# A Trainium2 residual block: the casts of the mixer's first weight blocks moved three units later and one unit later

## The chip, the cores and the metric

The kernel runs on one core of a Trainium2 chip. The metric is the device time of one execution in microseconds (us), median over runs. The core has five engines that run their own instruction queues in order: TensorE (PE in the profile, its weight loads PEld), VectorE (DVE), ScalarE (ACT), GpSimd (POOL) and SyncE (SP). In this kernel SP only issues loads from and stores to HBM; POOL issues accumulating transfers and does a few small operations.

## The reference

One layer of a streaming-encoder block on 512 rows of 1024 columns, all in float32:

```python
h = h + 0.5 * _swiglu(_rmsnorm(h, ffn1_norm[i]), ffn1_w_in[i], ffn1_w_out[i])
z = _rmsnorm(h, mix_norm[i]) @ w_in[i]
conv_a, conv_gt, q, k, v, r, g_lr = jnp.split(z, SPLIT_POINTS, axis=-1)
y_conv = _conv_module(conv_a, conv_gt, conv_w[i], conv_b[i], conv_ln_g[i], conv_ln_b[i])
y_gla = _gla(q, k, v, r, g_lr, gate_w_up[i], gate_b[i], gla_norm[i])
h = h + jnp.concatenate([y_conv, y_gla], axis=-1) @ w_out[i]
h = h + 0.5 * _swiglu(_rmsnorm(h, ffn2_norm[i]), ffn2_w_in[i], ffn2_w_out[i])
gate = jax.nn.sigmoid(_rmsnorm(h, ple_norm[i]) @ ple_w_gate[i])
h = h + gate * (p[i] @ ple_w_proj[i])
```

The SwiGLU layers have 2816 inner columns. `w_in` has 1024 rows; its columns 0 to 511 are conv_a (the value of the convolution's GLU), 512 to 1023 conv_gt (its gate), then come q, k, v, r and the low-rank gate. The change touches the passage from the first SwiGLU layer to the product with `w_in`.

## The kernel before, in words

**Products in three passes.** A float32 product is made of reduced-precision passes. Each operand is split in a high part (`act.copy` to float32r) and a low part (the difference), and `mm3` makes three matmuls: high by high, high by low, low by high. For weights the high part is cast by ACT (`high`), and the low part is made in one of two ways: by a DVE subtraction (`low`; `parts` is both steps), or by `added`: ACT writes the raw weights times -1, rounded like the high part, and POOL issues a transfer that adds the raw weights to it, which leaves raw minus high. Which way is taken is written at each place.

**Buffers.** A load (`load`, `fetch`, line 233, issued on SP) goes into a raw buffer `wr`; there are six in all. A raw buffer is free once its last reader is done: the DVE subtraction, or the landing of the POOL transfer. High and low parts of most weights go to `wh` and `wl`, six each. The first weight blocks of the mixer are made ahead by `ahead`: it loads 128 columns of all 1024 rows (512 KB) for each block and splits them with `high4` in two tiles of four row blocks each, into `big` tiles called `wa`, of which there are 20 in the pool that also holds rows and activations. So one block of 128 columns is one load, two casts and two ACT instructions by -1 of 128x512, and two POOL transfers of 256 KB; `ahead(w_in, c, 2 * P)` makes two blocks.

**The first SwiGLU layer.** `ffn` works on pairs of 256 inner columns, eleven in all (0 to 10), most of them with seven products of sums of blocks instead of eight (units m1, m2, m6, m7, m5, m4, m3). The result goes through the output weights in `second`, in cuts of the inner columns; the last cut, columns 16 to 21 in units of 128, is in two parts of three: a first half of units "last",0, 2, 4 and a second half of units "rest",0, 2, 4, 6 and 7, each for two column blocks of h and each with its own load of 384 KB. The last pair's order is m1, m2, m6, m7, m5, "last",0, m4, m3, "last",2, "last",4, "rest",0, "rest",2, "rest",4, "rest",6, "rest",7. Each of the "last" and "rest" units is 18 matmuls of 512 columns. The second half needs the activations of the last pair, made by `act_parts` from m3's result; the "rest" units finish two blocks of h each: DVE adds them to h, ACT makes the high part `hg` for the mixer, DVE its low part, ACT squares h and DVE adds the squares to `sqacc` (`norm.add`).

**Order.** `drive` writes the units down in turn: a unit's own jobs first (its load was ordered seven units ahead, its cast and subtraction are ordered four units ahead of it), then the first thing left by the unit before, the unit's products with its hook, and what else was left. `hooks` maps a unit to work that is put in at its end of products. In `piece` of `second` the hook comes after the h rows and their `hg` casts, and ahead of the low parts and squares. PE, DVE and ACT keep this order through `Ordered` (line 46), within one part of the kernel; the mixer begins a new order (`in_order(True)` at line 1053), and its instructions may be placed by the scheduler between those of the layer's end. SP and POOL have no such order written by hand: a load is issued in turn as soon as a buffer is free for it.

**The mixer's begin.** `wb, wa = w_ahead` takes the gate's first two blocks (wb, columns 512 to 767) and the value's first two (wa, columns 0 to 255). The products are `pb0` with wb[0], `pa0` with wa[0], `pb1` with wb[1], `pa1` with wa[1], 24 matmuls each. In pa0 stand the column sums of sqacc, from which the row scale comes; `spread` of it stands in pb1. Further weights (`raw_b`, `raw_a`, `raw_q`, `raw_k`) are loaded by SP behind wa, and cast by ACT into w2b, w2a, wq and wk.

Of the kernel before, what the change touches and what calls it, by code (L numbers as in the profile page):

```python
# [15 lines left out]
P = 128  # L16
SEQ = 512
D = 1024
DC = D // P
DFF = 2816  # L20
D_CONV = 512
# [41 lines left out]
def block_kernel(ctx: ExitStack, tc: tile.TileContext, a: dict, out: bass.AP):  # L63
# [26 lines left out]
    def bt2(dt=F32R, s="a"):  # L90
        t = big.tile([P, 2, SEQ], dt, tag="A", bufs=NA, name=nm(s))
        hi, lo = t[:, 0], t[:, 1]
        whole_of[id(hi)] = hi, t
        return hi, lo
# [133 lines left out]
    def raw(nk, ncol):  # L228
        return wp.tile([P, 1024], F32, tag="raw", bufs=6, name=nm("wr"))[:, :nk * ncol].rearrange(
            "p (k c) -> p k c", k=nk)  # L230

    def fetch(r3, src, k0, nk, c0, ncol):
        nc.sync.dma_start(out=r3, in_=src[k0 * P:(k0 + nk) * P, c0:c0 + ncol].rearrange("(k p) c -> p k c", p=P))

    def load(src, k0, nk, c0, ncol):
        r3 = raw(nk, ncol)
        fetch(r3, src, k0, nk, c0, ncol)
        return r3
# [16 lines left out]
    def added(w):  # L255

        h3, l3, r3 = w
        act.mul(l3, r3, -1.0)
        pool.dma_start(out=l3.bitcast(F32), in_=r3, accum_op=ALU.add)
        return w  # L260
# [10 lines left out]
    def ahead(src, c0, ncol):  # L271


        return [[added(w) for w in high4(load(src, 0, DC, c, P))] for c in range(c0, c0 + ncol, P)]

    def high4(r3):

        w = []
        for k in range(0, DC, 4):
            hi, lo = (t.rearrange("p (k c) -> p k c", k=4) for t in bt2(s="wa"))  # L280
            act.copy(hi, r3[:, k:k + 4])
            w.append((hi, lo, r3[:, k:k + 4]))
        return w
# [355 lines left out]
    def constants():  # L639
        _, cwrow, gwurow = made  # L640
        gwu = cp.tile([P, 2 * P], F32, name="gwu")
        act.copy(gwu, gwurow)
        cw = cp.tile([P, 4 * WIDTH], F32, name="cw")
        ps = aux()
        for c in range(4):
            pe.transpose(ps[:, c * WIDTH:(c + 1) * WIDTH], cwrow[:, c * P:(c + 1) * P], ident[:WIDTH, :WIDTH])
        dve.tensor_copy(cw, ps[:, 0:4 * WIDTH])
        mean = cp.tile([P, P], F32, name="mean")
        pool.memset(mean, 1.0 / D_CONV)
        m1, m2 = (bt(s="m1")[:, 0:4 * CH].rearrange("p (c t) -> p c t", t=CH) for _ in range(2))  # L650
        mask = cp.tile([P, 4, CH], I32, name="mask")
        pool.memset(m1, 1.0)
        pool.memset(m2, 1.0)
        pool.affine_select(out=m1, in_=m1, compare_op=ALU.is_gt, fill=0.0, base=0,
                           pattern=[[0, 4], [-1, CH]], channel_multiplier=1)
        pool.affine_select(out=m2, in_=m2, compare_op=ALU.is_gt, fill=0.0, base=-CH,
                           pattern=[[0, 4], [-1, CH]], channel_multiplier=1)
        pool.tensor_copy(mask[0:CH], m1[0:CH])
        pool.tensor_copy(mask[CH:P], m2[CH:P])
        nbias = cp.tile([P, 2], F32, name="nbias")  # L660
        for j in range(2):
            dve.tensor_scalar(nbias[:, j:j + 1], vec("gate_b", j), -1.0, None, ALU.mult)
        made[:] = cw, gwu, mean, mask, nbias
# [359 lines left out]
    w_in = a["w_in"][0]  # L1023
    w_ahead = []

    def sums_hooks(x, names, at):

        h = {}
        for name, key in zip(names, at):
# [6 lines left out]
                  ("h4", 1): lambda *_: [steps[4](), xb.split("t2")],  # L1036
                  ("h5", 1): lambda *_: [xb.split("t3"), w2.s12()]})
    hooks.update({("m5", 3): lambda *_: made[0](), ("m3", 3): lambda *_: constants(),
                  ("m4", 10): lambda *_: w_ahead.append(ahead(w_in, D_CONV, 2 * P)),
                  ("last", 4): lambda *_: w_ahead.append(ahead(w_in, 0, 2 * P))})  # L1040
    FAR = {("h5", 1): 3, ("m1", 2): 3}
    CASTS = {("h5", 1): 4, ("m1", 2): 4}
    ADDS = {("h4", 1), ("m2", 2)}
# [77 lines left out]
    rs, rsb = mid  # L1121
# [427 lines left out]
    for k in range(4):  # L1549
        for n in range(3):  # L1550
            w, ps = half[n]
# [329 lines left out]
    rs = norm.rows()  # L1881
# [98 lines left out]
```

## Time and profile before

| | |
|---|---|
| median of three runs | 934.96 us (933.71 to 935.58) |
| the profiled execution | 934.95 us |
| its span, first to last instruction | 933.1 us |
| granted TensorE clock, mean | 0.997 |
| HBM read and written | 93.61 MB, 2.10 MB |

In the rows of the timeline a line has its start in us from the span's begin, its length in us, the engine, the line of the kernel, the operation, output and input tiles by name with their shapes, the count, and in brackets the idle time of the engine before it and what ended that. All operations pass through one helper, line 46, so they are told apart by their tiles. In rows where several instructions are merged, the length is from the first's start to the last's end. Output `wa` is the high or low part of the mixer's first blocks (both wb and wa of the code have the tile name `wa`), `wr` a raw weight buffer, `act` the activations' parts, `hg` the parts of the rows for the next layer, `pd` and `ps` are accumulators.

### The profile page before, as it was taken

The page shows a single profiled execution, that of the slowest core. Times are in us where ns is not written, and L with a number is a line of the kernel's source. Part 1 is how long each engine was busy: PE and PEld are TensorE (multiplying, and loading weights), DVE is VectorE, ACT ScalarE, POOL GpSimd, SP SyncE. Part 2 cuts the span into 40 slices and gives each one's busy share as a digit, 9 for nine tenths or more (in the row PEclk, how much of TensorE's full clock was granted, in tenths as well). Part 3 has the DMA queues.
Part 4 walks back from the last instruction along what each step waited for, and adds up shares of the span by engine and source line. Part 5 has one row for each costly group of instructions (what it writes and reads, how often), then busy time and mean ns, then how long its engine had stood idle before and what let it go on. Part 6 is the DMA issues. An engine that isn't in the chain of part 4 may idle for free.

```text
span 933.1 us, 12990 instructions
## 1 busy us (share of the span) xinstructions
PE 923.0 (99%) x5011; PEld 785.3 (84%) x5011; DVE 826.6 (89%) x1107; ACT 509.7 (55%) x745; POOL 56.9 (6%) x74
## 2 busy tenths in 40 slices
PE   9999999999999999999999999999999999999996
PEld 7898888888888878788877889888888888888885
DVE  6799989999999776999987789999999999997896
ACT  5874445445544574463564875355445444456883
POOL 0100100000000021001030020000000000000131
PEclk9999999999999999999999999999999999999998
DMA  7643333233432594346552654333223422348463
GB/s 231 186 112 113 116 113 113 74 108 113 124 87 66 153 237 116 77 111 161 137 124 79 158 115 134 113 113 116 89 90 122 126 89 79 110 132 245 92 111 115
DMA packets 108129, 114.37 MB, mean 123 GB/s; under 512 B 5203, under 2 KB 96517, under 8 KB 108068
## 3 DMA queue, kind: packets, MB, share of 16 engines
q1 hardware_dynamic: 101748, 94.67, 33.0%
q0 software_dynamic: 6304, 18.88, 11.2%
q8 instruction: 39, 0.64, 0.3%
q14 instruction: 22, 0.18, 0.1%
q10 hardware_dynamic: 16, 0.00, 0.0%
HBM read 93.61 MB, written 2.10 MB: 103 GB/s over the span
## 4 chain that ended last, share of the span: by engine, by line
PE 96%; DVE 2%; ACT 1%; DMA 1%; issue 0%; POOLq 0%; DVEq 0%; ACTq 0%
PE ps L46 58%; PE pd L46 38%; DMA wr<-in_w_in 1%; DVE wl L46 1%; DVE sq L46 0%; DVE g L46 0%; ACT act L46 0%; ACT wa L46 0%; ACT wh L46 0%; DVE u L46 0%; DVE rs L46 0%; ACT yc L46 0%; DVE y L46 0%; DVE s L46 0%; DVE act L46 0%
## 5 line engine op out<-in xcount | busy, mean ns | idle before, releaser
L46 DVE TENSOR_TENSOR wl<-wr,wh 128x1024 fp32r<-128x1024 f32 (+2 forms) x161 | 188.6, 1182 | 18.6 <-ACT wh L46 18.5
L46 ACT CAST wh<-wr 128x1024 fp32r<-128x1024 f32 (+2 forms) x178 | 176.4, 1022 | 21.6 <-PE ps L46 6.4
L46 PE MATMUL pd<-hg,wh 128*128 128x512 f32 x576 | 150.0, 391 | 0.0
L46 PE MATMUL ps<-act,wh 128*128 128x512 f32 x448 | 138.8, 391 | 0.5 <-ACT act L46 0.3
L46 PEld LDWEIGHTS pd<-hg,wh 128*128 128x128 f32 x576 | 106.1, 188 | 20.7 <-DVE u L46 0.3
L46 PE MATMUL ps<-hg,wh 128*128 128x512 f32 (+1 forms) x448 | 117.7, 347 | 0.1
L46 PE MATMUL pd<-t,wh 128*128 128x512 f32 x392 | 98.3, 393 | 0.0
L46 PEld LDWEIGHTS ps<-act,wh 128*128 128x128 f32 x448 | 83.1, 188 | 17.7 <-ACT act L46 0.7
L46 ACT ACTIVATE s<-g 128x512 f32<-128x512 f32 x48 | 30.3, 632 | 117.7 <-DVE g L46 117.7
L46 ACT COPY sq<-pd 128x1024 f32<-128x1024 f32 x45 | 45.8, 1017 | 86.7 <-PE pd L46 52.4
L46 PEld LDWEIGHTS ps<-hg,wh 128*128 128x128 f32 x448 | 78.0, 190 | 11.7 <-issue 1.3
L46 PE MATMUL ps<-act,wl 128*128 128x512 f32 x224 | 87.2, 389 | 0.0
L46 PE MATMUL pd<-hg,wl 128*128 128x256 f32 (+1 forms) x544 | 83.9, 289 | 0.0
L46 PEld LDWEIGHTS pd<-hg,wl 128*128 128x128 f32 x544 | 75.9, 190 | 6.3
L46 PEld LDWEIGHTS pd<-t,wh 128*128 128x128 f32 x392 | 70.6, 189 | 12.5
L46 PE MATMUL ps<-hg,wl 128*128 128x512 f32 (+1 forms) x224 | 77.1, 344 | 0.0
L46 ACT CAST wh<-sm 128x1024 fp32r<-128x1024 f32 x42 | 44.1, 1051 | 57.1 <-DVE sm L46 50.9
L46 DVE SCALAR_TENSOR_TENSOR cv<-glu,cw,cv 128x502 f32<-128x502 f32 (+24 forms) x90 | 61.9, 734 | 0.3
L46 PEld LDWEIGHTS pd<-t,wl 128*128 128x128 f32 x392 | 53.5, 191 | 3.8
L46 DVE TENSOR_TENSOR sq<-pd,sq 128x1024 f32<-128x1024 f32 x45 | 54.8, 1219 | 0.8 <-PE pd L46 0.8
L46 DVE TENSOR_TENSOR wl<-sm,wh 128x1024 fp32r<-128x1024 f32 x42 | 51.1, 1220 | 5.0 <-ACT wh L46 5.0
L46 PE MATMUL ps<-wh,hg 128*128 128x512 f32 x176 | 54.8, 393 | 0.0
(322 smaller groups left out, 1638.5 us busy)
## 6 DMA issues: line engine op xcount, KB each, us to landing
wr<-in_ffn_w_in SPq DMA_DIRECT2D x84, 512.0 KB
wr<-in_ffn_w_out SPq DMA_DIRECT2D x32, 512.0 KB
wr<-in_w_in SPq DMA_DIRECT2D x20, 512.0 KB
wl<-wr POOLq DMA_DIRECT2D x18, 512.0 KB, 5.2
wr<-in_ffn_w_out SPq DMA_DIRECT2D x16, 384.0 KB
wr<-in_w_out SPq DMA_DIRECT2D x8, 512.0 KB
wq<-in_ple_w_gate SPq DMA_DIRECT2D x8, 512.0 KB
wl<-wq POOLq DMA_DIRECT2D x8, 512.0 KB, 4.6
```

Source lines behind the costliest of these rows:

```text
L46: inst = call(*args, **kwargs)
```

## The change

The first two blocks (wb) are still loaded in the hook of m4 of pair 10, but only loaded. Their casts, the instructions by -1 and POOL's transfers come in the hook of "last",4, three units later. The other two blocks (wa), loads and all, go from the hook of "last",4 to that of "rest",0, the first unit of the second half. The number of instructions of every kind is the same.

```diff
@@ -271,7 +271,11 @@
     def ahead(src, c0, ncol):
 
 
-        return [[added(w) for w in high4(load(src, 0, DC, c, P))] for c in range(c0, c0 + ncol, P)]
+        return prepared([load(src, 0, DC, c, P) for c in range(c0, c0 + ncol, P)])
+
+    def prepared(rs):
+
+        return [[added(w) for w in high4(r3)] for r3 in rs]
 
     def high4(r3):
 
@@ -1036,8 +1040,9 @@
                   ("h4", 1): lambda *_: [steps[4](), xb.split("t2")],
                   ("h5", 1): lambda *_: [xb.split("t3"), w2.s12()]})
     hooks.update({("m5", 3): lambda *_: made[0](), ("m3", 3): lambda *_: constants(),
-                  ("m4", 10): lambda *_: w_ahead.append(ahead(w_in, D_CONV, 2 * P)),
-                  ("last", 4): lambda *_: w_ahead.append(ahead(w_in, 0, 2 * P))})
+                  ("m4", 10): lambda *_: w_ahead.append([load(w_in, 0, DC, D_CONV + i * P, P) for i in range(2)]),
+                  ("last", 4): lambda *_: w_ahead.append(prepared(w_ahead.pop())),
+                  ("rest", 0): lambda *_: w_ahead.append(ahead(w_in, 0, 2 * P))})
     FAR = {("h5", 1): 3, ("m1", 2): 3}
     CASTS = {("h5", 1): 4, ("m1", 2): 4}
     ADDS = {("h4", 1), ("m2", 2)}
```

One thing beside the places: before, each block's load was followed by its own casts; after, `ahead` writes both loads first and then the casts of both.

## The prediction, made before the changed kernel ran

> **What bounds the kernel now.** I read the totals first, then TensorE by unit, then the chain of waits around the change, and last the rows of ScalarE (ACT), VectorE (DVE), SP and TensorE (PE) there.
>
> ```profile
> span 933.1 us, 12990 instructions
> PE 923.0 (99%) x5011; PEld 785.3 (84%) x5011; DVE 826.6 (89%) x1107; ACT 509.7 (55%) x745; POOL 56.9 (6%) x74
> ```
>
> PE is busy for 923.0 of 933.1 us, so only what makes PE wait can be won. The units around the edit, as stretches of PE time (start:end, length, PE busy and count, clock, DMA share, GB/s):
>
> ```profile
> 322.27:330.46 8.19, 8.19 (x39) 1.00 0.80 140
> 330.46:335.61 5.15, 4.66 (x19) 1.00 1.13 281
> ```
>
> The first row is units "last",2 and "last",4, two times 18 matmuls: 4.10 us a unit. The second is "rest",0, with as many matmuls, and it takes 5.15: 1.05 us are lost. The clock is 1.00 in both. The chain of waits says why (start, length, what):
>
> ```profile
> 318.42 5.70 DMA wr<-in_w_in
> ...
> 326.34 0.73 ACT wh L46
> ...
> 327.10 0.96 DVE wl L46
> 328.06 0.61 DVE g L46
> ...
> 329.30 0.95 DVE wl L46
> 330.26 0.61 DVE m L46
> ...
> 330.89 0.63 ACT act L46
> ...
> 331.55 0.70 DVE act L46
> ```
>
> The load of the second w_in block holds ACT; behind it stand the cast for "rest",2, m3's silu path (g, m) and the splits of the last pair's activations, which "rest",0 reads from its fourth matmul on. ACT's own rows:
>
> ```profile
> 318.84 1.14 ACT L46 CAST wa<-wr 128x512 fp32r<-128x512 f32 x2 [2.42 <-DMA wr<-in_w_in]
> ...
> 324.15 1.14 ACT L46 CAST wa<-wr 128x512 fp32r<-128x512 f32 x2 [3.11 <-DMA wr<-in_w_in]
> ...
> 326.25 0.82 ACT L46 CAST wh<-wr 128x768 fp32r<-128x768 f32 x1
> 326.97 0.57 ACT L46 COPY g<-pd 128x512 f32<-128x512 f32 x1
> ...
> 333.46 1.14 ACT L46 CAST wa<-wr 128x512 fp32r<-128x512 f32 x2 [0.69 <-DMA wr<-in_w_in]
> ...
> 337.64 1.77 ACT L46 CAST wh<-wr 128x768 fp32r<-128x768 f32 x2
> ```
>
> There is a second place. "rest",7 ends at 351.93, where the mixer's first block begins:
>
> ```profile
> 351.93 6.52 PE L46 MATMUL ps<-hg,wa 128*128 128x512 f32 x27
> 358.40 1.05 PE L46 MATMUL ps<-ones,sqacc 128*128 128x1 f32 x8
> ```
>
> 27 matmuls at 4.10/18 = 0.228 us are 6.15, so PE could reach the column sums of sqacc at 358.08; it starts them at 358.40. DVE is the one that is late there:
>
> ```profile
> 322.39 0.69 DVE L46 TENSOR_TENSOR m<-u,s 128x512 f32<-128x512 f32 x1
> 327.10 0.96 DVE L46 TENSOR_TENSOR wl<-wr,wh 128x768 fp32r<-128x768 f32 x1 [4.02 <-ACT wh L46]
> ...
> 338.50 0.96 DVE L46 TENSOR_TENSOR wl<-wr,wh 128x768 fp32r<-128x768 f32 x1 [4.74 <-ACT wh L46]
> ...
> 343.24 0.69 DVE L46 TENSOR_TENSOR sqacc<-sqacc,sq 128x512 f32<-128x512 f32 x1
> ...
> 345.05 1.22 DVE L46 TENSOR_TENSOR wl<-wr,wh 128x1024 fp32r<-128x1024 f32 x1
> ...
> 348.10 1.22 DVE L46 TENSOR_TENSOR wl<-wr,wh 128x1024 fp32r<-128x1024 f32 x1
> ...
> 356.86 1.49 DVE L46 TENSOR_TENSOR sqacc<-sqacc,sq 128x512 f32<-128x512 f32 x2
> ```
>
> From the first sqacc addition (343.24) to the end of the last (358.35) DVE needs 15.1 us of new rows h, their splits hg, sqacc, and two weight subtractions of the mixer (345.05 and 348.10). This second chain is as tight as PE itself, and the change moves work in front of it.
>
> **The change, part by part.**
>
> *Wait taken from m4.* The loads for wb stay in m4's hook; the eight ACT instructions and four POOL transfers go to "last",4, past the jobs of m3, "last",2 and "last",4. ACT then meets "rest",2's cast with nothing ahead of it. What times the path is m3's products, which end with the start of "last",2 at 322.27, as PE does now. From the same rows' durations: copy g about 322.5 to 323.05; DVE, after m ends at 323.08, subtracts for "rest",2 to 324.0, two g steps (0.61 each and some 0.1 between) to 325.3, the subtraction for "rest",4 to 326.2; silu is ready by then; m to 326.9; two ACT splits (0.63 and 0.5) to 328.0, DVE's part to 328.8. PE wants these at its fourth matmul, 330.46 + 3 x 0.228 = 331.14, so 2.3 us are spare. **Removed: the whole 1.05 us of "rest",0.** Bounds: nothing, if something else holds ACT by 2.3 us and more; 1.05 at most. I take 1.05.
>
> PE idle before two of its matmuls adds up to 0.49 us only, since the profile shows the overlapped ones longer. The Trainium skill (Perfetto Trace Analysis, § Identifying the Most-Contended Engine) says that matmul busy time is a poor measure because matmuls are pipelined. By idle time this term would be 0.49, and by the starts 1.05; the row of 5.15 against 4.10 is what I go by.
>
> *wb's casts in "last",4.* Eight instructions take 337.64 - 333.46 = 4.2 us when nothing holds them. ACT: "rest",6's cast to 328.7 (0.82), wb to 332.9, then "rest",7's cast to 333.7; its DVE subtraction ends at 334.6 instead of 339.4, 4.8 us earlier. PE ends "rest",0 at 330.46 + 4.10 = 334.56, so DVE adds its rows h at 334.6 to 335.8. wb has landed long before: its loads are issued at
>
> ```profile
> 314.96 0.37 SPq L233 DMA_DIRECT2D wr<-in_w_in  x1
> 318.42 0.37 SPq L233 DMA_DIRECT2D wr<-in_w_in  x1
> 319.29 0.37 SPq L233 DMA_DIRECT2D wr<-in_ffn_w_out  x1
> 327.59 1.11 SPq L233 DMA_DIRECT2D wr<-in_w_in  x2
> ```
>
> and the casts of 318.84 and 324.15 show them landed 3.9 and 5.7 us later. The four POOL transfers now leave between 330 and 334. Their landing time:
>
> ```profile
> wa<-wr POOLq DMA_DIRECT2D x4, 256.0 KB, 7.8
> ```
>
> So wb is complete near 342, and its first matmul is at 351.93 - 1.05 = 350.9: hidden with 9 us of cover. Cost 0.
>
> The Trainium skill (DMA: Bandwidth & Descriptors, § Anatomy of one DMA — SWDGE (gpsimd) path) has 2.0 us plus bytes over 436 GB/s for such a transfer, an estimate of 2.6 us here. This row has three times that, with DMA engines full. By the page wb's two raw buffers would be free 5 us sooner and the slower rival below would lose most of its chance; the trace is what I use.
>
> *wa's loads and casts in "rest",0.* SP issues a load when a raw buffer is free, and the hook only sets its rank. wa's two loads follow "rest",7's on SP (319.29). In the old order wa's first load left at 327.59; now the buffers of "rest",2 and "rest",4 are free at about 324.0 and 326.2, so wa lands by 332 at the latest (5.7 us). Its casts stand behind the two hg casts of "rest",0 (0.7 each, 335.2 to 336.5), with no wait: 336.5 to 340.7. Behind them stand the two squares of "rest",0, to 341.8, and DVE waits for those before sqacc. POOL issues wa's transfers by 341; with 7.8 us they land at 349, and PE reads wa first after wb's 24 matmuls, at 350.9 + 24 x 0.228 = 356.4: hidden, 7 us of cover. Past these numbers each late microsecond would cost PE as much.
>
> *What sets the end then.* DVE's first sqacc starts at about 341.8 instead of 343.24; plus 15.1 it ends at 356.9. PE, earlier by 1.05, wants it at 358.08 - 1.05 = 357.03. So the most that can be won here is 1.05 + 0.32 = 1.37 us. The mixer's own casts are spread over ACT's gaps between these:
>
> ```profile
> 339.87 1.05 ACT L46 CAST wh<-wr 128x1024 fp32r<-128x1024 f32 x1 [0.46 <-PE pd L46]
> 340.83 1.33 ACT L46 ACTIVATE hg<-h,vcol 128x512 fp32r<-128x512 f32 x2
> 342.07 0.61 ACT L46 ACTIVATE sqacc<-h 128x512 f32<-128x512 f32 x1
> 342.59 0.62 ACT L46 ACTIVATE sq<-h 128x512 f32<-128x512 f32 x1
> 343.67 1.05 ACT L46 CAST wh<-wr 128x1024 fp32r<-128x1024 f32 x1 [0.47 <-DMA wr<-in_w_in]
> ```
>
> If one of them (1.0 us) is placed ahead of "rest",0's hg, sqacc starts at 342.8, ends at 357.9, and 0.5 is left. Bounds: +0.5 to +1.37 won; I take 1.0, between them.
>
> **Sum.** 934.95 (the profiled execution's own time; the median of the three runs, 934.96, is the same) - 1.0 = **933.95 us**; with the bounds 933.3 to 934.6. The span would be 932.1.
>
> **Rivals.**
>
> *Nothing gained.* sqacc starts at 343.2 as before, because ACT's 4.2 us for wa are paid in front of it and one or two mixer casts too; then PE's 1.05 us reappear as a longer wait ahead of the column sums. For it: DVE is the late one there already. Against it: "rest",7's subtraction comes 4.8 us sooner. Time 934.9.
>
> *Slower: a cast of the next weights stands on ACT ahead of "rest",0's hg.* wb's raw buffers are held until its accumulation lands, near 339 to 342 rather than 327.6 to 331.9, so the loads of w2b and w2a move back. Now both w2b casts stand ahead of that hg (the casts at 338.4 and 339.87). If they stay there, the second load leaves when "rest",7's buffer is free (334.6) and lands at 338.5 to 340.3 (3.9 to 5.7 us); its cast ends at 341.4, hg at 342.7, wa at 346.9, the squares at 348.0, sqacc at 363.1 instead of 358.35: 4.7 us slower, 939.7. With half of that, 937.3. It decides from a first sqacc later than 345.1, which is 343.24 + 1.87. For it: ACT already waited 0.47 at such a cast. Against it: the order on ACT between the two parts is made when the program is scheduled, and casts whose load comes later tend to be put later.
>
> *The loads of wa are late.* Before, wa's first load waited for wb's accumulation:
>
> ```profile
> SPq L233 <- DMA wa<-wr: 10.9, 2, 7.8
> ```
>
> If wa still takes wb's buffers, its loads leave near 339 and 341, the second lands by 347, its four casts (2.1 us) and the squares (1.1) end at 350.2: sqacc ends at 365.3, 6.9 us late, 941.9. Against it: "rest",2 and "rest",4 are now cast ahead of wb, so their buffers come first. This would also be the case of a change that doesn't do what it says.
>
> *More than forecast.* PE waits once more, late in the mixer:
>
> ```profile
> 504.03 0.70 DVE lnsq L46
> ...
> 504.75 0.82 ACT yc L46
> ```
>
> If DVE's weight subtractions leave its full stretch, for the time in which it waits for the column sums, the taps may end sooner and up to these 1.52 us go too: 934.95 - 1.37 - 1.52 = 932.1. Nothing in the edit aims there.
>
> **How the numbers follow.** Forecast 0.40, nothing gained 0.15, cast ahead of hg 0.28, wa's loads late 0.09, more than forecast 0.08. A measurement of this kernel tells about 0.2% (1.87 us, the spread of the three runs) from no change. Faster by more than that means under 933.09: the last case and 0.12 of the forecast, 0.20. Slower means over 936.83: 0.21 of the 0.28 and the 0.09, 0.30. Within: 0.50. The range for 8 in 10 goes from 932.8 to 938.0; it leaves out the top of the third case, the fourth and the lowest end. The likeliest case alone has 933.3 to 934.6.
>
> **What would show it.** Right: no ACT wait on in_w_in between 315 and 330; "rest",0 in 4.1 us of PE; "rest",7's subtraction at about 334; wa's eight ACT instructions after the first two hg, without a wait on DMA; a first sqacc near 342. Wrong: a first sqacc past 343.2, an ACT cast waiting on in_w_in between 334 and 346, wa's loads leaving SP after 330, or a PE wait ahead of the column sums of more than 0.3 us.

## The result and the profile after

| | us |
|---|---|
| before, median of 9 runs | 934.96 (933.71 to 935.58) |
| changed, median of 9 runs | 937.27 (935.90 to 938.40) |
| ratio, 95% interval | 1.0025 (1.0015 to 1.0035) |
| changed, the profiled execution | 935.90, span 934.0 |

The change makes the kernel slower, by 0.25% of the median, where a gain of 1.0 us was forecast (933.95 us). The measured median still lies in the stated range of 932.8 to 938.0. The profiled execution is the fastest of the nine; it lies 0.95 us over that of before (934.95), and its span 0.9 us over (934.0 against 933.1). The page and the stretches of "last",2 with "last",4 and of "rest",0 in the changed kernel:

```profile
span 934.0 us, 12995 instructions
PE 923.3 (99%) x5011; PEld 785.5 (84%) x5011; DVE 826.5 (88%) x1107; ACT 509.6 (55%) x745; POOL 56.9 (6%) x74
```

```profile
322.25:330.44 8.19, 8.19 (x39) 6.77 (x38) 6.63 (x10) 5.63 (x10) 0.00 (x0) 1.00 0.53 150
330.44:334.52 4.08, 4.08 (x20) 3.38 (x19) 0.94 (x2) 4.04 (x7) 3.53 (x4) 1.00 0.95 220
```

"rest",0 now takes 4.08 us instead of 5.15: the stall is gone. It comes back, and more, in the mixer's first block. TensorE of the changed kernel from the end of "rest",7:

```profile
350.61 0.39 PE L46 MATMUL ps<-act,wl 128*128 128x512 f32 x1
351.43 4.34 PE L46 MATMUL ps<-hg,wa 128*128 128x512 f32 x18 [0.44 <-ACT wh L46]
356.31 0.50 PE L46 MATMUL ps<-hg,wa 128*128 128x512 f32 x1 [0.53 <-ACT hg L46]
357.10 2.10 PE L46 MATMUL ps<-hg,wa 128*128 128x512 f32 x8 [0.29 <-DVE hg L46]
359.15 1.05 PE L46 MATMUL ps<-ones,sqacc 128*128 128x1 f32 x8
```

The last "rest" matmul starts at 350.61, so with 0.23 us a matmul the unit ends at 350.84, against 351.93 before. From there to the column sums it is 8.31 us, against 358.40 - 351.93 = 6.47 before. Won 1.09, lost 1.84: the column sums start at 359.15, 0.75 us later than before. The chain of waits, followed back from there, shows what PE waited for:

```profile
333.13 6.33 DMA wa<-wr
339.47 0.02 SPq L233
...
339.52 10.78 DMA wr<-in_w_in
...
350.38 1.05 ACT wh L46
351.42 0.64 ACT hg L46
...
352.08 1.42 DVE hg L46 x2
```

A transfer that accumulates wb's low part lands at 339.47 and frees a raw buffer; the load for the second w2a block leaves then and takes 10.8 us; its cast on ACT comes ahead of the `hg` of "rest",4. ACT's rows:

```profile
332.73 1.93 ACT L46 CAST wh<-wr 128x768 fp32r<-128x768 f32 x2
335.18 1.34 ACT L46 ACTIVATE hg<-h,vcol 128x512 fp32r<-128x512 f32 x2 [0.53 <-DVE h L46]
336.42 1.13 ACT L46 CAST wa<-wr 128x512 fp32r<-128x512 f32 x2
...
341.70 1.05 ACT L46 CAST wh<-wr 128x1024 fp32r<-128x1024 f32 x1
344.63 1.05 ACT L46 CAST wh<-wr 128x1024 fp32r<-128x1024 f32 x1 [1.88 <-DMA wr<-in_w_in]
345.58 1.33 ACT L46 ACTIVATE hg<-h,vcol 128x512 fp32r<-128x512 f32 x2
...
350.38 1.05 ACT L46 CAST wh<-wr 128x1024 fp32r<-128x1024 f32 x1 [2.42 <-DMA wr<-in_w_in]
351.33 1.33 ACT L46 ACTIVATE hg<-h,vcol 128x512 fp32r<-128x512 f32 x2
```

The two w2a casts (344.63, 350.38) wait 1.88 and 2.42 us for their loads, and right behind each stands the `hg` of a "rest" unit. ACT met the same order before, but its casts there waited 0.47 and 1.36 us:

```profile
348.36 1.05 ACT L46 CAST wh<-wr 128x1024 fp32r<-128x1024 f32 x1 [1.36 <-DMA wr<-in_w_in]
350.56 1.34 ACT L46 ACTIVATE hg<-h,vcol 128x512 fp32r<-128x512 f32 x2 [1.15 <-DVE h L46]
```

The second of these casts cost nothing before: the `hg` behind it waited 1.15 us more for its rows h. VectorE of the changed kernel, which needs `hg` for the low part:

```profile
333.58 0.96 DVE L46 TENSOR_TENSOR wl<-wr,wh 128x768 fp32r<-128x768 f32 x1 [3.94 <-ACT wh L46]
...
341.75 0.69 DVE L46 TENSOR_TENSOR sqacc<-sqacc,sq 128x512 f32<-128x512 f32 x1 [3.56 <-ACT sq L46]
...
346.33 1.41 DVE L46 SCALAR_TENSOR_TENSOR hg<-h,vcol,hg 128x512 fp32r<-128x512 f32 x2 [1.56 <-ACT hg L46]
...
352.08 1.42 DVE L46 SCALAR_TENSOR_TENSOR hg<-h,vcol,hg 128x512 fp32r<-128x512 f32 x2 [0.80 <-ACT hg L46]
...
357.62 1.48 DVE L46 TENSOR_TENSOR sqacc<-sqacc,sq 128x512 f32<-128x512 f32 x2
```

Its first sqacc starts at 341.75, 1.49 us earlier than before, and its last ends at 359.10, 0.75 us later. The stretch grew from 15.1 to 17.35 us, by the two new waits of 1.56 and 0.80.

Why do the loads land late? The six loads that follow wb's on SP are, in the code's order, wa's two, w2b's two and w2a's two. The leaving times, before (the last three) and then changed (the first two and the last three):

```profile
332.31 1.00 SPq L233 DMA_DIRECT2D wr<-in_w_in  x1
333.79 1.30 SPq L233 DMA_DIRECT2D wr<-in_w_in  x1
344.05 0.37 SPq L233 DMA_DIRECT2D wr<-in_w_in  x1
```

```profile
323.96 0.37 SPq L233 DMA_DIRECT2D wr<-in_w_in  x1
326.16 0.37 SPq L233 DMA_DIRECT2D wr<-in_w_in  x1
...
335.98 0.37 SPq L233 DMA_DIRECT2D wr<-in_w_in  x1
336.44 1.37 SPq L233 DMA_DIRECT2D wr<-in_w_in  x1
339.52 0.37 SPq L233 DMA_DIRECT2D wr<-in_w_in  x1
```

wa's leave earlier than before (327.59 and 328.09 there). The second w2b load leaves 3.7 us later (335.98 against 332.31), the first w2a load 2.65 us later (336.44 against 333.79): SP stands 5.8 us before the second w2b load for a buffer that wb's accumulation still reads. The second w2a load leaves 4.5 us earlier than before and lands later nonetheless: 10.8 us, where before it had left at 344.05 and was cast at 348.36. The DMA queues from 330 to 352, q1 the loads of SP, q0 the transfers of POOL (packets, MB, their time as a share of 16 engines' span), before and then changed:

```profile
q1 hardware_dynamic: 8967, 4.53, 80.0%
q0 software_dynamic: 659, 1.19, 31.2%
```

```profile
q0 software_dynamic: 1152, 2.10, 54.3%
q1 hardware_dynamic: 5935, 3.00, 50.2%
```

The shares sum to over 100% in both: the DMA engines are full. wb's four transfers, which had left at 320.8 to 327.9 before, now leave at 330.5 to 334.4 and lie in this full stretch. POOL moves 0.91 MB more in it, the loads 1.53 MB less.

### The profile page after: what moved, and what is told of

It is laid out like the page before. It is cut to its first block, busy times and chain, and to the rows that moved or that the text cites. A ratio compares the mean times of both kernels' runs of the same rounds, so it can differ in the third digit from the quotient of the medians.

```text
span 934.0 us, 12995 instructions
## 1 busy us (share of the span) xinstructions
PE 923.3 (99%) x5011; PEld 785.5 (84%) x5011; DVE 826.5 (88%) x1107; ACT 509.6 (55%) x745; POOL 56.9 (6%) x74
## 4 chain that ended last, share of the span: by engine, by line
PE 93%; DMA 2%; issue 2%; DVE 1%; ACT 1%; POOL 0%; POOLq 0%; DVEq 0%; ACTq 0%; SPq 0%
PE ps L46 57%; PE pd L46 37%; DMA wr<-in_w_in 2%; DMA wa<-wr 1%; DVE wl L46 0%; DVE hg L46 0%; ACT wh L46 0%; DVE g L46 0%; ACT hg L46 0%; DVE sqacc L46 0%; DVE sq L46 0%; ACT act L46 0%; POOL wa L46 0%; DVE u L46 0%; DVE rs L46 0%
```

## The experiments

The theories: **L**, late loads: the casts for w2a stand on ACT in front of `hg` and wait for loads that land late. **C**, the clock or some other cause in the later parts. **D**, which some expectations name: DVE needs a fixed time from the first sqacc to the last, whatever the loads do. Within L: **H**, hold: the loads leave late, because wb's raw buffers are held until its accumulation lands. **T**, traffic: the loads are slowed in flight by wb's and wa's accumulating transfers, which now share the full DMA engines with them.

| kernel | median us (runs) | ratio to before (95%) | profiled: us, span, column sums at |
|---|---|---|---|
| changed, again | 936.97 (6) | 1.0030 (1.0018 to 1.0042) | 937.14, 935.3, 360.47 |
| wb's part alone | 943.11 (4) | 1.0095 (1.0080 to 1.0111) | 943.15, 941.4, 366.60 |
| wa's part alone | 938.12 (4) | 1.0040 (1.0026 to 1.0054) | 938.87, 936.9, 362.10 |
| w2a casts held back | 933.98 (11) | 0.9995 (0.9986 to 1.0004) | 933.67, 931.6, 356.83 |
| the same, repeated | 934.00 (11) | 0.9993 (0.9985 to 1.0002) | 933.87, 931.8, 356.97 |
| the same on the kernel before | 934.34 (11) | 0.9997 (0.9988 to 1.0005) | 934.58, 932.5, 357.73 |
| wb's low parts by DVE | 935.26 (10) | 1.0009 (1.0000 to 1.0018) | 934.94, 933.2, 358.32 |
| the same, wb's raw buffers held | 935.41 (10) | 1.0009 (0.9999 to 1.0018) | 935.46, 933.7, 358.82 |
| wa's low parts by DVE | 934.78 (10) | 1.0003 (0.9993 to 1.0012) | 934.61, 932.8, 357.91 |

The kernel before ran beside them with medians of 934.45 (the first four rows), 934.73 (the repeat, its twin on the kernel before, and the next two) and 934.68 us (the last).

**The changed kernel again**, for the spread of 2.5 us in its runs.

> The changed kernel as it is, for a second profile and more times. Theory L (two casts of the next mixer weights stand on ACT ahead of rows' hg and wait for their loads): 936 to 938.4 us again, with ACT waits on in_w_in of 1.9 and 2.4 us or more at the casts near 342 to 350 us, longer ones in a longer execution, and column sums of sqacc at 359.1 or later. Theory C (a lower granted clock in the longer runs makes the 1.4 us between the profiled 935.9 and the median 937.3): the waits are as in the first profile and PE rows are longer somewhere else.

ACT's casts of w2b[1], w2a[0] and w2a[1] in this second profile:

```profile
342.27 1.06 ACT L46 CAST wh<-wr 128x1024 fp32r<-128x1024 f32 x1 [0.67 <-DMA wr<-in_w_in]
346.54 1.05 ACT L46 CAST wh<-wr 128x1024 fp32r<-128x1024 f32 x1 [3.21 <-DMA wr<-in_w_in]
350.79 1.05 ACT L46 CAST wh<-wr 128x1024 fp32r<-128x1024 f32 x1 [0.92 <-DMA wr<-in_w_in]
```

The same casts wait, 4.8 us in sum instead of 4.3, otherwise divided: the first w2a load left at 336.31, nearly as in the first profile, and took 10 us instead of 8. sqacc starts at 341.63, as there, but the column sums come 1.32 us later, and the span is 1.3 us longer. So DVE's stretch starts at the same time and the landing of loads sets its end, which speaks against D. PE is busy for 7.25 us from 350 to 360 where the first profile has 8.75; from 360 to 600 both have the same 239.77. The clock was 1.00 in all these stretches, so C has no part in the difference between the two profiles. For the longest runs C stays open. Of the fifteen runs of this kernel, the six with a mean granted clock of 0.995 or 0.996 are those of 937.85 us and more; the other nine, at 0.997 or 0.998, took 937.27 us or less. None of the six was profiled.

**wb's part alone**: wb is cast in "last",4, and wa stays in the same hook.

```diff
-                  ("last", 4): lambda *_: w_ahead.append(prepared(w_ahead.pop())),
-                  ("rest", 0): lambda *_: w_ahead.append(ahead(w_in, 0, 2 * P))})
+                  ("last", 4): lambda *_: [w_ahead.append(prepared(w_ahead.pop())), w_ahead.append(ahead(w_in, 0, 2 * P))]})
```

> Only wb's casts are late; wa's loads and casts stay in the hook of 'last',4, behind wb's. On ACT both w2b casts then stand ahead of the first hg, and both w2a casts ahead of the second pair of hg. Theory L: unit 'rest',0 takes 4.1 us of PE, but the second w2a load lands near 350 as in the changed kernel, so the second pair of hg starts near 351 instead of 344.6 and the column sums near 365: about 941 us. Rival D (DVE's stretch of fixed length from the first sqacc to the last, loads not to blame): first sqacc near 343 to 344, 934 to 935.5.

943.11 us, even more than expected, and at another cast: the second of w2b.

```profile
347.44 1.05 ACT L46 CAST wh<-wr 128x1024 fp32r<-128x1024 f32 x1 [8.30 <-DMA wr<-in_w_in]
348.40 1.33 ACT L46 ACTIVATE hg<-h,vcol 128x512 fp32r<-128x512 f32 x2
```

Its load left at 336.51, when an accumulation of wb had landed (336.37), and took 10.8 us. All `hg` stand behind it, from that of "rest",0 on: the first sqacc moves to 350.81, past the 343 to 344 that D would have. The mechanism holds; the place was expected wrongly.

Part of this loss is the clock. TensorE waited 7.36 us ahead of the mixer's first block, and from 356 to 362 its granted clock was 0.50. The block's first 27 matmuls took 7.76 us (358.84 to 366.60) in place of 6.15, so some 1.6 of the 8.2 us by which the column sums are later than in the kernel before are slower matmuls. Here the low clock came behind a long wait; whether the same happened in the long runs of the changed kernel no profile shows.

**wa's part alone**: wb as before in m4, wa in "rest",0.

```diff
-                  ("m4", 10): lambda *_: w_ahead.append([load(w_in, 0, DC, D_CONV + i * P, P) for i in range(2)]),
-                  ("last", 4): lambda *_: w_ahead.append(prepared(w_ahead.pop())),
+                  ("m4", 10): lambda *_: w_ahead.append([[added(w) for w in high4(load(w_in, 0, DC, c, P))] for c in range(D_CONV, D_CONV + 2 * P, P)]),
```

> Only wa's loads and casts are moved, to 'rest',0; wb is loaded and cast in m4 as before. On ACT the second w2b cast stands between the first two hg, and both w2a casts ahead of the second pair. Theory L: 'rest',0 keeps its 5.15 us; the second w2a load lands near 349.4 as before the change, so the second pair of hg starts near 350.4 and the column sums near 364: about 940.5 us. Rival D: first sqacc at 342 to 343, about 934.5.

938.12 us, 2.4 less than expected. The first w2b cast waits ahead of the first `hg`, again for a load that had left only when an accumulation of wb had landed (332.06):

```profile
337.42 1.05 ACT L46 CAST wh<-wr 128x1024 fp32r<-128x1024 f32 x1 [3.64 <-DMA wr<-in_w_in]
```

The subtraction for it stands on DVE ahead of the new rows h, waits too, and so holds up the first `hg`. The first sqacc starts at 347.89, and the w2a casts wait for nothing. So the change's first half alone is worse than both together, and the second half alone is no better. What matters is the time at which a load gets a buffer, against the place at which its cast stands on ACT.

**The w2a casts held back**: the first is ordered behind the last square of the layer's end, and its subtraction goes behind pa0, to that of the second. No load or transfer is moved by hand. The second kernel with this edit is a repeat, the third has it on the kernel before.

```diff
+    last_square = act.latest
...
     w2a = [high(raw_a[0])]
+    act.behind(act.latest, last_square)
...
-    low(w2a[0])
     pa0 = zblock(wa[0], hg, {1: lambda: mid.append(rsqrt_mean(colsum([norm.acc]), D, TB))})
+    low(w2a[0])
```

> The changed kernel with the two w2a casts held behind the last square of the layer on ACT, and their two subtractions behind the row scale on DVE; nothing else moves in either order. Theory L: no ACT wait on in_w_in before 355 us, first sqacc still at 341.8, last one done near 355.7, PE without a wait from 330 to the column sums near 357.0: 1.37 us below the kernel before, 933.6 us, and the runs as close together as those of before. Rival D, or a late wb or wa: 936 to 937, with the column sums past 358.4.

> The changed kernel with the two w2a casts held back, once more beside the kernel before on the same chip, since its first interval against the kernel before reached over 1. Theory L: 0.4 to 1.4 us below the kernel before, PE without a wait from 330 us to the column sums.

> The kernel before, with the same two w2a casts held behind the layer's last square and their subtractions behind the row scale; wb and wa stay as before. It shows what the order alone is worth. Theory L: 'rest',0 keeps 5.15 us of PE, the wait ahead of the column sums (0.3 us) goes; about 0.35 us below the kernel before, 934.1 us, and 0.5 to 1.05 above the same order in the changed kernel. Rival: the order alone does all of it, and this kernel is as fast as the other (within 0.2 us).

With the edit on the changed kernel ACT has the last `hg` ahead of both w2a casts:

```profile
352.21 1.34 ACT L46 ACTIVATE hg<-h,vcol 128x512 fp32r<-128x512 f32 x2 [1.82 <-DVE h L46]
354.50 1.98 ACT L46 CAST wh<-wr 128x1024 fp32r<-128x1024 f32 x2
```

and PE has no wait left in the mixer's begin; the chain of waits from 318 to 362 is PE alone:

```profile
317.86 12.61 PE pd L46 x63
330.48 4.08 PE ps L46 x18
334.56 8.16 PE pd L46 x36
342.72 19.31 PE ps L46 x89
```

sqacc starts at 341.62 (341.75 in the changed kernel) and ends at 355.78, so the stretch is 14.2 us instead of 17.35. The column sums move from 359.15 to 356.83, and the median from 937.27 and 936.97 to 933.98: so with this edit the whole loss is gone. The edit does a second thing: it takes one subtraction of 1.2 us out of DVE's stretch. The kernel before tells the two apart. There the same edit shortens the stretch from 15.1 to 14.2 us (342.87 to 357.03), by 0.95. Of the 3.15 us won here, 2.2 are then left for the casts' place, as much as the 2.25 by which the change had made the stretch longer. On the kernel before, the same edit brings the column sums to 357.73, with the stall in "rest",0 still there. Between the two kernels with the edit, the change is worth 0.9 and 0.8 us at the column sums, and 0.34 us in the medians (934.34 against 934.00, which ran together), less than the 0.5 to 1.05 us that were expected. This is the fastest version measured, some 0.5 to 0.7 us under the kernel before, but its intervals reach over 1, so a gain isn't established.

**wb's low parts by DVE**, without POOL's transfers for wb: less traffic, and wb's buffers come free sooner. The w2b and w2a casts are kept at their places by `act.behind`, behind the squares of the same "rest" unit as in the changed kernel; the lines for that are left out of this diff and the next two.

```diff
-                  ("last", 4): lambda *_: w_ahead.append(prepared(w_ahead.pop())),
+                  ("last", 4): lambda *_: w_ahead.append([[low(w) for w in high4(r3)] for r3 in w_ahead.pop()]),
...
```

> The changed kernel with wb's low parts made by four DVE subtractions instead of four ACT instructions and four POOL transfers; the order of all other ACT instructions is held as in the changed kernel, the two w2a casts ahead of hg included. wb's raw buffers are free near 333 us instead of 336 to 339.5, and 1 MB less goes through the accumulating transfers. Theory H (the w2a loads are late because the raw buffers are held): they leave by 336 and land by 342, no ACT wait on in_w_in at the casts near 342 to 350, 933.5 to 934.2 us. Theory T (the DMA engines are full, whoever holds a buffer): they leave early and still land at 343.5 or later, waits of 1 us and more stay, 935 to 937.

The w2a loads left at 331.94 and 332.81, 4.5 and 6.7 us earlier than in the changed kernel: it was wb's accumulation that had held their buffers. No w2a cast waits, and 935.26 us is 2 us less than the changed kernel's 937.27. It missed the 933.5 to 934.2 that was expected, because a w2b cast now came ahead of the first `hg` and waited; its subtraction, which DVE waited 1.96 us for, stands between two new rows h and held up the second:

```profile
334.26 1.05 ACT L46 CAST wh<-wr 128x1024 fp32r<-128x1024 f32 x1 [2.92 <-DMA wr<-in_w_in]
```

**The same, with wb's raw buffers held**: two small ACT copies read them again behind wa's casts.

```diff
-                  ("rest", 0): lambda *_: w_ahead.append(ahead(w_in, 0, 2 * P))})
+                  ("rest", 0): lambda *_: [w_ahead.append(ahead(w_in, 0, 2 * P))] + [act.copy(warm, r3[:, 0, 0:1]) for r3 in held]})
...
```

> As the kernel with wb's low parts on DVE, same order, but ACT reads one column of each of wb's two raw buffers again behind wa's casts, so that they stay taken until about 340.8 us. No accumulating transfers for wb. Theory H: the first w2a load leaves after 340.8 and lands at 345 to 347, an ACT wait of 3 us and more, column sums past 360, 937 to 938.5. Theory T: without wb's 1 MB of transfers the loads land within 4 us, an ACT wait of 2 us at most, 935 to 936.5.

The hold took effect at other loads than meant: the first w2a load got another buffer and left at 336.78. As a test of H it is inconclusive. But the second w2a load left at 342.38, 2.9 us later than in the changed kernel, and was cast at 348.49 after a wait of 0.68, 1.9 us earlier: it took 6.1 us in place of 10.8. The DMA engines were emptier only before it left (0.43 from 336 to 342, against 1.03); while it was under way they were about as full (1.07 from 342 to 348, against 1.14), with wa's transfers beside it in both. It also left later, so this is no clean test of T either.

**wa's low parts by DVE** tells H and T apart: wb, its accumulations and its buffers stay as in the changed kernel, so the loads leave at the same times; only wa's 1 MB of transfers, which leave at 338.4 and later, is gone. The casts are kept in place as above.

```diff
-                  ("rest", 0): lambda *_: w_ahead.append(ahead(w_in, 0, 2 * P))})
+                  ("rest", 0): lambda *_: w_ahead.append([[low(w) for w in high4(r3)] for r3 in
+                                                          [load(w_in, 0, DC, i * P, P) for i in range(2)]])})
...
```

> The changed kernel with wa's low parts made by four DVE subtractions instead of four ACT instructions and four POOL transfers; wb, its buffers and its transfers stay as they are, and ACT's order is held as in the changed kernel. The w2a loads then leave when they did (336.4 and 339.5 us; only wa's own buffers come free sooner, which the later loads use), but 1 MB of accumulating transfers is gone from the stretch from 338 to 348. Theory T (full DMA engines make the landing late): the first w2a load lands by 343 and the second by 346 to 347, the ACT waits on in_w_in shrink below 1 us each, column sums at 357 to 358.4, 934 to 935. Theory H (late leaving alone): the same landings as in the changed kernel, 344.6 and 350.4, and since ACT comes to these casts earlier, waits of 2 us and more; column sums at 358.5 to 360, 936 to 937.

```profile
342.15 1.05 ACT L46 CAST wh<-wr 128x1024 fp32r<-128x1024 f32 x1 [2.65 <-DMA wr<-in_w_in]
343.98 1.06 ACT L46 CAST wh<-wr 128x1024 fp32r<-128x1024 f32 x1 [0.77 <-DMA wr<-in_w_in]
344.94 1.33 ACT L46 ACTIVATE hg<-h,vcol 128x512 fp32r<-128x512 f32 x2
347.21 1.04 ACT L46 CAST wh<-wr 128x1024 fp32r<-128x1024 f32 x1
```

The loads left at 335.95, 336.41 and 339.04, as in the changed kernel (335.98, 336.44, 339.52). The second w2a load landed by 347.2 instead of 350.3, in at most 8.2 us where the two profiles of the changed kernel have 10.8 and 11.8, and its cast waits for nothing: without wa's transfers it isn't late. That is T, with one correction: the DMA engines were no emptier, 1.17 from 342 to 348 against 1.14. Later loads, which left earlier in this run, filled them, and they held this load up less than POOL's transfers had. The first landed at 343.9 in 7.5 us, against 8.1 and 10.1 in the two profiles of the changed kernel, and ACT still waited for it and for the second w2b load (2.65 us, where ACT arrived sooner). Both had left late, which is hold, though how much of their flight is traffic this run can't tell. For the first w2a load the kernel before helps: there it left at 333.79 and was cast at 343.67, after 9.8 us, no sooner than the 8.1 and 10.1 us here. So what the change did to this load is that it leaves 2.65 us later, and what it did to the second, which took 4.2 us before, is mostly traffic. Both theories have a share. More raw buffers, which would take the hold alone away, weren't tried, so the first half of this is argued from the rows and not tested.

## Why the prediction was wrong

**Wait taken from m4: right.** Forecast 1.05 us off "rest",0, measured 5.15 to 4.08. ACT has no wait on in_w_in between 315 and 330.

**wb's casts and wa's loads: right.** wa's loads left at 323.96 and 326.16 (forecast 324.0 and 326.2), "rest",7's subtraction ran at 333.58 (forecast about 334), wa's casts from 336.42 without a wait (forecast 336.5). wb's accumulation landed at 339.47 (forecast 339 to 342), and PE didn't wait for it. The Trainium skill's rule for such a transfer (DMA: Bandwidth & Descriptors, § Anatomy of one DMA — SWDGE (gpsimd) path), an estimate of 2.6 us, doesn't fit: the last of wb's four took 6.33 us, as the chain shows.

**DVE's first sqacc: right.** Forecast 341.8, measured 341.75.

**The failed step: "What sets the end then".** It added a fixed 15.1 us to the first sqacc, and took the mixer's own casts at 1.0 us of ACT each, at most one of them in front. Measured 17.35 us (341.63 to 360.41, that is 18.8, in the second profile). A cast standing in an in-order queue costs until its load has landed, not its own duration. The row at 343.67 was quoted: a cast with a wait of 0.47 us for a load. What I didn't do was to carry the later leaving of loads, worked out in the slower rival, on to that cast and to the one behind it, nor to add wb's 1 MB to the DMA engines that the quoted row had at 1.13. Two of the prediction's own signs of being wrong came: a cast that waited on in_w_in ahead of 346 (344.63), and waits of PE ahead of the column sums (1.26 us in the rows above).

**The slower rival named the mechanism and missed the place and the size.** It had a cast of the next weights ahead of an `hg`, raw buffers held by wb's accumulation, and the loads moved back; it put this at the w2b casts and the `hg` of "rest",0, and took the first sqacc as the test. By that test it hadn't come true (341.75, under 345.1), and the loss came one and two units later, at w2a. The rival as written is what wb's part alone does: first sqacc at 350.81, 943.11 us, against the rival's 939.7; it had the second w2b load leave at 334.6 and land by 340.3, where it left at 336.51 and was cast at 347.44. Its 937.3 for half the delay is near the median of 937.27, by a partial coincidence, since the working was another.

**The argument against it was half right.** The scheduler did put a w2b cast behind `hg` (341.70), but no rule keeps a cast behind in general: the w2a casts kept the place they had before.

**What the forecast's gain is worth.** With the casts held back the column sums come at 356.83, so PE's 1.05 + 0.32 us are to be had there (forecast 357.03), with a subtraction moved as well. The median gains less than that, 0.5 to 0.7 us. Spans have a median of 931.9 against 932.65 to 932.9 for the kernel before, so they gain 0.75 to 1.0; the profiled execution of the kernel before, on which the forecast was worked out, had a longer span (933.1) than its median. The rest lies outside the span, below.

## What to carry to other kernels

A cast moved to a later place takes with it the release of its raw buffer and its accumulating transfer: list the loads that wait for that buffer, find where their casts stand in the in-order queue, and price those casts by the landing of their loads. Where a cast for later work stands ahead of work on the path, try ordering it behind by hand; here that alone took the loss away. Look at what else moves through a full DMA stretch: with 1 MB of accumulating transfers taken out of it, the two w2a loads landed in 7.5 and at most 8.2 us instead of 8.1 to 11.8, though the engines' busy share stayed about the same.

## What the runs showed of the hardware

- **The packets of accumulating transfers took more of the DMA engines' time per byte than those of loads.** From 330 to 352 of the changed kernel POOL's 2.10 MB took 54.3% of the engines' time and the loads' 3.00 MB 50.2%: 25.9% a MB against 16.7%, a factor of 1.55. In the same stretch of the kernel before the factor is 1.48. Since the shares add up to more than 100%, these times overlap, and the factor isn't a pure cost.
- **A load of 512 KB took between 3.9 and 11.8 us to land**: 3.9 for the one that left at 314.96 in the kernel before, 10.8 for the one at 339.52 in the changed kernel, 11.8 for the same load in its second profile (338.91). SP's issue itself, 0.37 us in most rows, took 1.0 to 1.4 us in three rows of the full stretch (332.31, 333.79, 336.44).
- **The granted clock halved behind a long wait of TensorE.** With wb's part alone TensorE waited from 351.5 to 358.84, and its clock was 0.50 from 356 to 362. In the other profiles, whose waits there are shorter (2.60 us the longest, with wa's part alone), it stayed at 1.00 in this place.
- **The time outside the span differs between kernels**: medians of 1.79 us for the kernel before, 1.95 for the changed kernel, 2.1 with the casts held back, 1.74 with the buffers held. It takes back some 0.3 us of what the span gains; why, no run here shows.
